# Low parts of the gating and GLU weights: a VectorE subtraction becomes a ScalarE negation and an accumulating DMA

## The chip, the cores and the metric

The kernel runs on one core of one Trainium2 chip. The metric is device time in microseconds (us) of one execution, the median over several runs. The engines are TensorE (PE in the profile; its weight loads are PEld), VectorE (DVE), ScalarE (ACT), GpSimd (POOL) and SyncE (SP). Sixteen DMA engines move data between HBM and SBUF for all queues.

## The reference

One decoder layer over 1024 prompt positions and 64 sample tokens (1088 columns), D_MODEL 1024, all in float32:

```
p     = rmsnorm(x) @ w_in                      # 1024 -> 512 (S5) + 512 (u) + 512 (v)
y     = gelu(Re(C h) + D u)                    # S5: 32 groups, 64 complex states, a scan over positions
o_s5  = y * sigmoid(y @ w_glu + b_glu)         # GLU, 512 x 512
v     = layernorm(gelu(p_v));  u = gelu(p_u)
o_cm  = u * (tril(W_s) v + b)                  # gating, 8 heads, chunks of 128 positions
x     = x + concat(rmsnorm(o_s5), rmsnorm(o_cm)) @ w_out
x     = x + (silu(h @ w_gate) * (h @ w_up)) @ w_down,  h = rmsnorm(x)
```

The last hidden states, the last v rows and a final RMSNorm are outputs too.

## The kernel before, in words

Activations lie with features on the 128 partitions and the 1088 columns in three chunks of 384, 384 and 320. Every large product is made of three matmuls on rounded parts: a float32 operand is split in a high part, `hi`, of type float32r, and a low part `lo = src - hi`. `mm3` (lines 150 to 152) adds `hi*hi`, `hi*lo` and `lo*hi` in one PSUM bank. So each weight tile is split once after it has been loaded. `split` does that in two instructions: ScalarE copies to `hi` (line 146) and VectorE subtracts (line 147). The two form the low part strictly one after the other, and `lo` is a tile that TensorE waits for.

`w_in` comes as six column quarters `q` of 256 columns, each in two halves of 512 rows. `load_q` (lines 239 to 245) loads a half of 512 KB to a raw tile of which three exist (`raw`, shared by most weight loads), and splits it. The halves live in three slots (`wqp`, tags `wqh` and `wql`; the tile `cwr` in the profile), so that the slot of a half is free only when TensorE has read another half for the last time. Quarters 0 and 1 are the S5 group's inputs (`s5_in`), 2 and 3 are the v columns (`v_quarter`, tile `pv`), 4 and 5 the u columns (`cm_out`, tile `pu`). In all of these the first half (k of 0 to 3) is read before the second (k of 4 to 7).

The S5 group is worked off in eight steps (`s5_a`, `s5_b`, `s5_c`): VectorE builds tables and scans, TensorE makes small products, and the halves of the partitions are swapped by DMA (`Sw`, `gw`). TensorE does the products of v and u between them, and VectorE the layer norm of v and the gating. When the last S5 step has stored its `ys`, four loads bring the result back by features (tile `g`, line 761, through `ys_d`), and the GLU begins (`glu`, tile `pg`). The GLU's weight tiles `wgh` and `wgl` lie in memory that the S5 steps have used, so they are written only then, from raw tiles that were loaded long before (lines 754 to 757). The output projection (`wo_tile`) and the feed-forward part follow.

The program is written as one stream, and a planner orders each engine's queue at build by estimated times of its instructions and by what is ready (`schedule_with_timeline_sim=True`); within a queue the chip keeps that order. All DMAs are issued by SyncE; GpSimd issues none.

Of the kernel before, what the change touches and what calls it, by code (L numbers as in the profile page):

```python
# [10 lines left out]
F32 = mybir.dt.float32  # L11
F32R = mybir.dt.float32r
I32 = mybir.dt.int32
AF = mybir.ActivationFunctionType
ALU = mybir.AluOpType
# [68 lines left out]
def layer_kernel(ctx: ExitStack, tc: tile.TileContext, A, O, dbg=None):  # L84
    nc = tc.nc
    V, S, P, PE, Q = nc.vector, nc.scalar, nc.gpsimd, nc.tensor, nc.sync
# [51 lines left out]
    def raw(name, shape):  # L138
        n = int(np.prod(shape))
        t = rawp.tile([128, 1024], F32, tag="raw", name=name, bufs=3)[:, :n]  # L140
        if len(shape) == 2:
            t = t.rearrange("p (a b) -> p a b", a=shape[0])
        return t

    def split(src, hi, lo, eng=None):
        S.activation(hi, src, AF.Copy)  # L146
        return (eng or V).tensor_tensor(lo, src, hi.bitcast(F32), ALU.subtract)  # L147

    def mm3(p, wh, wl, ah, al, start, stop):
        PE.matmul(p, wh, ah, start=start, stop=False)  # L150
        PE.matmul(p, wh, al, start=False, stop=False)  # L151
        return PE.matmul(p, wl, ah, start=False, stop=stop)  # L152
# [86 lines left out]
    def load_q(key, src, to=None):  # L239

        r = raw(f"w{key[0]}{key[1]}{key[2]}", (4, 256))
        Q.dma_start(r, src)
        h, l = to or [wqp.tile([128, 4, 256], F32R, tag=x, name=x) for x in ("wqh", "wql")]
        split(r, h, l)
        WQ[key] = (h, l)

    def load_wq(q):
        for half in range(2):
            load_q(("i", q, half), A["w_in"][q, :, 4 * half:4 * half + 4, :])
# [33 lines left out]
    def fm_group(q, c, tag="mm"):  # L283

        n0, n = CH[c]
        pp = [bank(f"pu{m}", tag)[:, :n] for m in range(2)]
        km = [(k, m) for k in range(8) for m in range(2)]
        for k, m in km if q == 0 else sorted(km, key=lambda x: x[1]):
            wh, wl = wq(q, k, slice(128 * m, 128 * m + 128))
            MM[q, c] = mm3(pp[m], wh, wl, xh[:, k, n0:n0 + n], xl[:, k, n0:n0 + n], k == 0, k == 7)  # L290
        return pp
# [14 lines left out]

    load_x(0, 0)
    load_q(("i", 0, 0), A["w_in"][0, :, 0:4, :])
    load_x(0, 1)
    load_q(("i", 0, 1), A["w_in"][0, :, 4:8, :])  # L310
    load_x(0, 2)
    load_x(0, 3)
# [298 lines left out]
    r = raw("bdr", (8, 64))  # L611
# [16 lines left out]
    r = raw("wsr", (8, 128))  # L628
# [4 lines left out]
    for q in range(2):  # L633
# [3 lines left out]
        for i in range(4):  # L637
            m, h = divmod(4 * q + i, 2)
# [6 lines left out]
    def v_quarter(q, j):  # L645
        p = bank("pv")
        for k in range(8):
            wh, wl = wq(q, k, slice(0, 256))
            mm3(p[:, 0:256], xh[:, k, tok(j)], xl[:, k, tok(j)], wh, wl, k == 0, k == 7)
        S.activation(v[:, j, 256 * (q - 2):256 * (q - 1)], p[:, 0:256], AF.Gelu_apprx_tanh, scale=r1c[:, j:j + 1])  # L650
# [101 lines left out]
    wgh = gl.tile([128, 4, W], F32R, name="wgh")  # L752
    wgl = gl.tile([128, 4, W], F32R, name="wgl")
    for i in range(2):
        r = raw(f"wg{i}", (2, W))
        Q.dma_start(r, A["w_glu"][:, 2 * i:2 * i + 2, :])
        split(r, wgh[:, 2 * i:2 * i + 2, :], wgl[:, 2 * i:2 * i + 2, :])
    G5 = []
    for m in range(4):
        g5 = gl.tile([128, 8, 136], F32, name=f"g5{m}")  # L760
# [10 lines left out]
    def glu(c):  # L771
        n0, n = CH[c]
        acc = ACC5[c] = gl.tile([128, 384], F32, tag="acc", name="acc", bufs=3)[:, :n]
        for m in range(4):
            p = bank("pg", "s5" if m % 2 else "mm")
            for k in range(4):
                mm3(p[:, :n], wgh[:, k, 128 * m:128 * m + 128], wgl[:, k, 128 * m:128 * m + 128],
                    xh[:, k, n0:n0 + n], xl[:, k, n0:n0 + n], k == 0, k == 3)
            sg = gl.tile([128, 384], F32, tag="sg", name="sg", bufs=2)[:, :n]
            S.activation(sg, p[:, :n], AF.Sigmoid, bias=gcol("bglu", m))  # L780
            for z, s_, q_ in tc2n(G5[m], n0, n, sg, accum_to(gl, acc, m == 0)):
                V.tensor_tensor(z, z, s_, ALU.mult)
                S.activation(q_, z, AF.Square)
            accum_end(acc, m == 0)
# [32 lines left out]
    i = 0  # L817
# [522 lines left out]
```

## Time and profile before

| | |
|---|---|
| median of 3 runs | 1118.43 us (1116.59 to 1118.62) |
| the profiled execution | 1114.1 us, span 1112.3 us |
| PE busy | 1055.7 us, 95% |
| DVE busy | 894.6 us, 80% |
| ACT busy | 436.8 us, 39% |
| POOL busy | 322.3 us, 29% |
| DMA moved | 131.20 MB, mean 118 GB/s |

The profiled execution is one that the hardware profiler recorded; its span runs from the first to the last instruction. Busy shares are means over stages with different limits. Matmuls are pipelined and their recorded durations overlap, so a busy TensorE is not one at its peak. In lists of waits, the name behind the arrow is what ended the idle time.

### The profile page before, as it was taken

What the parts mean: (1) busy time and instruction counts of PE and PEld (TensorE: products, weight loads), DVE (VectorE), ACT (ScalarE), POOL (GpSimd) and SP (SyncE); (2) the same over time, 40 slices, a digit from 0 to 9 for tenths busy, and PEclk for the clock granted to TensorE, in tenths of its full rate; (3) what the DMA queues carried; (4) which work ended last, traced back from release to release, by engine and by line L of the source; (5) the groups of instructions that cost most, each with busy time, mean ns of one, the idle gap of its engine ahead of it and who ended that gap; (6) DMA issues with size and microseconds to landing.
All of it is one profiled execution on the core that took longest, in us unless ns stands there. A gap on an engine that the chain in (4) does not pass through costs nothing.

```text
span 1112.3 us, 20465 instructions
## 1 busy us (share of the span) xinstructions
PE 1055.7 (95%) x7966; PEld 1028.5 (92%) x7966; DVE 894.6 (80%) x1820; ACT 436.8 (39%) x834; POOL 322.3 (29%) x287
## 2 busy tenths in 40 slices
PE   7899999979999899999999999999999899999995
PEld 6799998869999789999999999999998899899994
DVE  7988999898988996666666666666669879879998
ACT  7314423477444543233233233233244334424561
POOL 5010350000000435425425435335335221223220
PEclk9999999989999899999999999999999999999997
DMA  8341334364223113223223223223256715514304
GB/s 278 105 145 48 96 111 144 82 195 168 96 94 111 39 57 128 90 77 127 77 91 127 75 81 124 88 74 128 82 183 213 277 39 197 174 50 141 127 15 161
DMA packets 81520, 131.20 MB, mean 118 GB/s; under 512 B 8976, under 2 KB 60048, under 8 KB 81296
## 3 DMA queue, kind: packets, MB, share of 16 engines
q1 hardware_dynamic: 81424, 129.91, 36.0%
q8 instruction: 62, 1.02, 0.4%
q14 instruction: 34, 0.28, 0.1%
HBM read 90.43 MB, written 34.24 MB: 112 GB/s over the span
## 4 chain that ended last, share of the span: by engine, by line
PE 65%; DVE 18%; DMA 8%; issue 4%; ACT 3%; POOL 1%; SPq 0%; DVEq 0%; ACTq 0%; POOLq 0%
PE u L152 15%; PE u L150 15%; PE u L151 15%; DMA h<-hid_d 4%; PE po L152 3%; PE po L151 3%; PE po L150 3%; DVE xl L147 2%; PE pv L151 1%; PE pv L150 1%; PE pv L152 1%; DVE cwr L147 1%; DVE fb L147 1%; DMA gw<-gt 1%; PE pg L150 1%
## 5 line engine op out<-in xcount | busy, mean ns | idle before, releaser
L150 PE MATMUL u<-xh,h 128*128 128x272 f32 x516 | 149.1, 289 | 1.7 <-ACT h L146 1.5
L152 PE MATMUL u<-xh,h 128*128 128x272 f32 x516 | 148.5, 289 | 1.3 <-DVE h L147 1.3
L151 PE MATMUL u<-xl,h 128*128 128x272 f32 x516 | 148.7, 289 | 0.8 <-DVE xl L147 0.8
L150 PE MATMUL u<-xh,fb 128*128 128x272 f32 x382 | 110.7, 290 | 0.6 <-DVE x1r L1134 0.4
L151 PE MATMUL u<-xl,fb 128*128 128x272 f32 x382 | 110.6, 290 | 0.6 <-DVE xl L147 0.6
L152 PE MATMUL u<-xh,fb 128*128 128x272 f32 x382 | 110.3, 290 | 0.0
L1049 POOL TENSOR_TENSOR tS<-q,q 128x512 f32<-128x512 f32 x22 | 29.4, 1338 | 245.5 <-DVE h L914 145.9
L150 PEld LDWEIGHTS u<-xh,h 128*128 128x128 f32 x516 | 97.1, 188 | 2.4 <-ACT h L146 1.9
L152 PEld LDWEIGHTS u<-xh,h 128*128 128x128 f32 x516 | 96.9, 188 | 1.7 <-DVE h L147 1.7
L151 PEld LDWEIGHTS u<-xl,h 128*128 128x128 f32 x516 | 97.2, 188 | 1.0 <-DVE xl L147 1.0
L146 ACT ACTIVATE h<-q 128x512 fp32r<-128x512 f32 (+1 forms) x83 | 51.0, 615 | 80.7 <-PE u L151 75.2
L147 DVE TENSOR_TENSOR h<-q,h 128x512 fp32r<-128x512 f32 (+1 forms) x83 | 69.1, 834 | 7.0 <-ACT h L146 5.7
L151 PEld LDWEIGHTS u<-xl,fb 128*128 128x128 f32 x382 | 72.5, 190 | 0.9 <-DVE xl L147 0.9
L150 PEld LDWEIGHTS u<-xh,fb 128*128 128x128 f32 x382 | 72.3, 189 | 1.0 <-DVE x1r L1134 0.6
L152 PEld LDWEIGHTS u<-xh,fb 128*128 128x128 f32 x382 | 72.2, 189 | 0.1
L150 PE MATMUL pu<-xh,cwr 128*128 128x384 f32 (+1 forms) x192 | 65.6, 346 | 6.2 <-DVE us L303 6.2
L1087 ACT ACTIVATE st<-st 128x272 f32<-128x272 f32 x88 | 37.8, 431 | 72.1 <-DVE st L1109 34.5
L152 PE MATMUL pu<-xh,cwr 128*128 128x384 f32 (+1 forms) x192 | 64.9, 341 | 0.0
L151 PE MATMUL pu<-xl,cwr 128*128 128x384 f32 (+1 forms) x192 | 64.7, 338 | 0.0
L1054 POOL TENSOR_TENSOR tS<-tS,q 128x512 f32<-128x512 f32 x22 | 30.4, 1383 | 113.2 <-DVE h L147 60.5
L146 ACT ACTIVATE fb<-q 128x512 fp32r<-128x512 f32 (+1 forms) x64 | 38.7, 608 | 56.9 <-PE u L151 49.0
L150 PE MATMUL u<-cwr,h 128*128 128x272 f32 x189 | 55.1, 291 | 2.9 <-ACT cwr L146 2.3
(439 smaller groups left out, 3741.7 us busy)
## 6 DMA issues: line engine op xcount, KB each, us to landing
hid_d<-st SPq DMA_DIRECT2D x22, 952.0 KB, 4.2
h<-hid_d SPq DMA_DIRECT2D x28, 544.0 KB, 3.9
q<-in_w_gate_dram SPq DMA_DIRECT2D x22, 512.0 KB, 3.5
q<-in_w_up_dram SPq DMA_DIRECT2D x22, 512.0 KB, 3.5
q<-in_w_d_dram SPq DMA_DIRECT2D x16, 512.0 KB, 3.8
wo<-in_w_out_dram SPq DMA_DIRECT2D x14, 512.0 KB, 4.2
wi<-in_w_in_dram SPq DMA_DIRECT2D x12, 512.0 KB, 5.7
h<-hid_d SPq DMA_DIRECT2D x14, 408.0 KB, 3.1
```

Of the source, the lines that this page charges most:

```text
L146: S.activation(hi, src, AF.Copy)
L147: return (eng or V).tensor_tensor(lo, src, hi.bitcast(F32), ALU.subtract)
L150: PE.matmul(p, wh, ah, start=start, stop=False)
L151: PE.matmul(p, wh, al, start=False, stop=False)
L152: return PE.matmul(p, wl, ah, start=False, stop=stop)
L1049: P.tensor_tensor(tS, a21, a22, ALU.add)
L1054: P.tensor_tensor(tS, tS, a11, ALU.subtract)
L1087: S.activation(dst, src, AF.Silu)
```

## The change

For the four halves each of v and u (quarters 2 to 5, eight halves) and for the two halves of the GLU's weights, the low part is made in another way. ScalarE writes `hi` as before, then ScalarE writes `-hi` into `lo`, and then GpSimd issues a DMA that reads the weights from HBM once more and adds them to `lo`. VectorE's subtraction falls away for these ten. Quarters 0 and 1, the output projection and the activations keep `split`.

```
+    def wsplit_d(raw_, src, hi, lo):
+        S.activation(hi, raw_, AF.Copy)
+        S.activation(lo, hi.bitcast(F32), AF.Copy, scale=-1.0)
+        P.dma_start(lo, src, accum_op=ALU.add)
...
     def load_q(key, src, to=None):
         r = raw(f"w{key[0]}{key[1]}{key[2]}", (4, 256))
         Q.dma_start(r, src)
...
-        split(r, h, l)
+        if key[0] == "i" and key[1] >= 2:
+            wsplit_d(r, src, h, l)
+        else:
+            split(r, h, l)
...
     for i in range(2):
         r = raw(f"wg{i}", (2, W))
         Q.dma_start(r, A["w_glu"][:, 2 * i:2 * i + 2, :])
-        split(r, wgh[:, 2 * i:2 * i + 2, :], wgl[:, 2 * i:2 * i + 2, :])
+        wsplit_d(r, A["w_glu"][:, 2 * i:2 * i + 2, :], wgh[:, 2 * i:2 * i + 2, :], wgl[:, 2 * i:2 * i + 2, :])
```

## Rows read from the trace of the kernel before

**Rows 1.** Busy time by stretch: start:end, us; then PE, PEld, DVE, ACT, POOL, PEclk, DMA share, GB/s.
```profile
30.00:72.00 42.00, 35.78 (x200) 34.35 (x199) 38.92 (x152) 10.72 (x19) 4.37 (x18) 0.92 0.27 85
72.00:161.00 89.00, 88.93 (x699) 85.17 (x698) 81.28 (x185) 30.58 (x73) 24.08 (x21) 1.00 0.37 102
161.00:219.00 58.00, 56.41 (x418) 50.67 (x416) 52.80 (x119) 23.07 (x54) 4.80 (x9) 1.00 0.41 115
219.00:230.00 11.00, 7.15 (x45) 4.87 (x44) 9.94 (x20) 6.51 (x10) 0.00 (x0) 0.84 0.37 113
230.00:264.00 34.00, 27.15 (x149) 26.84 (x149) 31.75 (x78) 28.95 (x62) 0.00 (x0) 0.90 0.54 169
```

**Rows 2.** The chain that ended last, 30 to 230 us: start, us on it, what.
```profile
40.96 1.14 DVE cwr L147
...
72.23 0.51 DVE cwr L147
...
85.07 0.12 PE pv L150
...
138.90 0.17 PE pu L151
...
164.07 1.14 DVE cwr L147
```

**Rows 3.** Waits of TensorE, 30 to 75 us: us in total, times, longest.
```profile
PE pu L150 <- DVE us L303: 6.2, 2, 5.2
```

**Rows 4.** Groups by line on VectorE, 72 to 230 us, shapes kept apart.
```profile
L147 DVE TENSOR_TENSOR cwr<-wi,cwr 128x1024 fp32r<-128x1024 f32 x7 | 8.5, 1215 | 0.5 <-ACT cwr L146 0.4
```

**Rows 5.** The GLU's raw weight tile: ns min/median/max, first and last start.
```profile
L146 ACT ACTIVATE wgh<-wg x2: 1046/1046/1046, 230.1 to 231.0; 128x1024 fp32r<-128x1024 f32 x2
L147 DVE TENSOR_TENSOR wgl<-wg,wgh x2: 1216/1217/1218, 232.2 to 233.8; 128x1024 fp32r<-128x1024 f32 x2
```

**Rows 6.** Timeline: split of the first and the last second half.
```profile
69.30 1.06 ACT L146 ACTIVATE cwr<-wi 128x1024 fp32r<-128x1024 f32 x1 [5.42 <-PE pu L151]
...
72.15 1.22 DVE L147 TENSOR_TENSOR cwr<-wi,cwr 128x1024 fp32r<-128x1024 f32 x1
...
178.12 1.04 ACT L146 ACTIVATE cwr<-wi 128x1024 fp32r<-128x1024 f32 x1
...
181.48 1.21 DVE L147 TENSOR_TENSOR cwr<-wi,cwr 128x1024 fp32r<-128x1024 f32 x1
```

**Rows 7.** Busy time by stretch around the GLU's start, columns as in the first group.
```profile
230.00:236.00 6.00, 0.00 (x0) 0.00 (x0) 6.00 (x13) 5.97 (x9) 0.00 (x0) 0.88 0.92 268
236.00:242.00 6.00, 5.15 (x18) 5.15 (x19) 5.98 (x15) 4.77 (x15) 0.00 (x0) 0.55 1.19 328
```

**Rows 8.** Timeline around the GLU's start: TensorE, then ScalarE.
```profile
218.76 0.31 PE L152 MATMUL pu<-xh,cwr 128*128 128x320 f32 x1
...
236.85 2.61 PE L150 MATMUL pg<-xh,wgh 128*128 128x384 f32 x7 [6.95 <-ACT xh L146]
...
239.58 0.52 PE L152 MATMUL pg<-xh,wgl 128*128 128x384 f32 x1
...
236.28 1.39 ACT L146 ACTIVATE xh<-g 128x384 fp32r<-128x384 f32 x4
238.10 1.39 ACT L146 ACTIVATE xh<-g 128x384 fp32r<-128x384 f32 x4 [0.44 <-DMA g<-ys_d]
```

**Rows 9.** DMA issues: KB each, median us to landing; the issue's own ns.
```profile
wi<-in_w_in_dram SPq DMA_DIRECT2D x12, 512.0 KB, 5.7
g<-ys_d SPq DMA_DIRECT2D x4, 544.0 KB, 7.2
L242 SPq DMA_DIRECT2D wi<-in_w_in_dram x12: 328/386/1387, 2.1 to 162.5; - x12
```

**Rows 10.** Timeline of GpSimd: one shape beside a busy VectorE.
```profile
148.14 1.29 POOL L710 TENSOR_TENSOR cvp<-v,lgb 128x512 f32<-128x512 f32 x1 [1.45 <-DVE v L658]
...
154.91 3.72 POOL L710 TENSOR_TENSOR cvs<-v,lgb 128x512 f32<-128x512 f32 x1 [2.53 <-DMA mb<-mb]
```

## The prediction, made before the changed kernel ran

> **What bounds the kernel now.** I read busy time by stretch first, then the chain that ended last, then the waits, and only then single instructions. Everything that the change touches lies between 40 and 245 us; what comes later is moved as a block. By stretch [rows 1] TensorE is full from 72 to 161 us (88.9 of 89.0) and nearly so to 219 (56.4 of 58.0); VectorE is close behind with 91% in both (81.3 of 89.0, 52.8 of 58.0). The chain [rows 2] says which of them counts where. Around 41 us it runs over VectorE, and a subtraction of a `w_in` half is on it with 1.14 us; TensorE waits there for VectorE, 5.2 us at the longest [rows 3]. From 85 us on the chain's pieces are matmuls, 0.12 us for one of `pv` and 0.17 us for one of `pu` [rows 2]. After 161 us it is VectorE's again: the subtraction at 164.07 is on it in full. TensorE ends its last `pu` at 219 us, and then idles before the GLU, 6.95 us in one piece [rows 8], while the last S5 step ends and its result comes back through HBM: from 236 to 242 us the DMA engines are as busy as they get (share 1.19, 328 GB/s) and TensorE has a mean clock of 0.55, so near its lower level of 1.2 GHz, after having idled [rows 7]. So there are three stages with different limits: VectorE before 72 us, TensorE with VectorE close behind it to 161, VectorE with S5 transfers to 230, and transfers around the GLU's start.
>
> **What the change removes.** Ten subtractions of 128x1024. One is the piece at 41 us. Seven lie between 72 and 230 us, 8.5 us in sum at 1.215 us each [rows 4]. Two are the GLU's, 1.217 us each, from 232.2 us on [rows 5].
> - The first: on the chain, TensorE waits at its end. Gain 1.1 us (bounds 0 and 1.2).
> - The five between 72 and 161 us (the first of them at 72.15 [rows 6]): 6.1 us of VectorE's time while TensorE has no gap. On the chain stands 0.51 us of them [rows 2], since the first of them delays a store that the S5 steps start from. What TensorE's order doesn't let through is no gain; but the S5 steps are also VectorE's work, and they end the stage at 230, after TensorE's last `pu`. Bounds 0.5 and 6.1; VectorE's 91% is nearer to the full than to nothing, TensorE's 100% to nothing, so I take half, 3.0 us.
> - The two at 164.07 and 181.48 (the latter with no idle of VectorE before it [rows 6]): on VectorE's part of the chain, 2.4 us (bounds 1.1 and 2.4).
> - The GLU's two: nothing. VectorE is busy there (6.00 of 6.00 us), but the stage waits for the `g` loads: the second one's split is released by the DMA [rows 7, 8].
> Sum of gains 1.1 + 3.0 + 2.4 = 6.5 us (1.6 to 9.7). The end of the S5 steps can move that far: there are 11 us between TensorE's last `pu` and 230 us.
>
> **What it adds.**
> - *Ten negations on ScalarE*, priced like the copy to `hi` of the same shape, 1.05 us [rows 5, 6]. From 72 to 219 us ScalarE is busy for a third (30.6 of 89, 23.1 of 58), so that idle time hides them; what is queued behind one on ScalarE is at worst an S5 evacuation, which TensorE and VectorE then wait for. Bounds 0 and 3.2 us (three that hit one); I take 0.5.
> - *Ten issues on GpSimd*, where no issue stands in this trace. An issue took SyncE 0.39 us [rows 9], and a GpSimd operation on 128x512 1.3 us [rows 10]: these are the bounds, and I take 1.3 us, being GpSimd's own. GpSimd is 27% busy to 161 us (24.1 of 89.0) and 8% after [rows 1], so the issues themselves cost nothing. But an issue waits for its negation, and the layer norm's small powers and the S5 states' copies are queued behind it on GpSimd, with VectorE and TensorE waiting for those; I count this with the low parts that come late.
> - *The low part comes later.* Now it ends 3.0 us after `hi` (70.36 to 73.37) and 3.5 us after it (179.16 to 182.69) in the first and the last of the four second halves [rows 6]. After the change: negation 1.05, issue 0.4 to 1.3, and the transfer, for which the nearest rows are a plain load of the same bytes, 5.7 us, and the loads of `g`, 7.2 us [rows 9]. That makes 7.1 to 9.6 us, so 4 to 6 us later. The four first halves have slots that come free early, or are read late. The four second halves are needed almost at once, since their slot is released by the matmuls just ahead. The cover: TensorE has the first-half products of the next groups, in four PSUM banks 4 x 12 matmuls, 5.8 us at 0.12 or 8.2 at 0.17 [rows 2]. If the planner puts these ahead, nothing is lost; if it keeps today's order, there are 12 matmuls (1.4 or 2.0 us) and TensorE stands still for up to 4 x 6 us. I take nothing, because interleaving is what this planner can do in a full stage; 24 us is the other end.
> - *The GLU's start.* The two accumulating DMAs can be issued from about 232 us, after `hi` is there, amid the `g` loads. They bring 2 x 0.524 MB more from HBM; at the 328 GB/s that the engines moved then [rows 7] this is 3.2 us of all sixteen, while `g` waits. Twice that, 6.4 us, if adding costs the engines a second pass over the bytes. `wgl` is first needed at 239.58 [rows 8], so lateness up to about 240 is covered, and the two negations on ScalarE (2.1 us, ScalarE 5.97 of 6.00 busy [rows 7], `g` split at 236.28 right behind other work [rows 8]) overlap with waiting for `g`. Bounds 1.0 and 6.4; a plain load is the nearest row, so I take 3.2.
>
> Such a transfer has no row here. The Trainium skill (DMA: Bandwidth & Descriptors, Anatomy of one DMA) gives about 2.0 us and bytes over 436 GB/s for a DMA issued by GpSimd, an estimate of 3.2 us for one of these; by it the low parts would be only some 2 us later than now and the sum would stay what it is. No run here shows it yet.
>
> **Sum.** -6.5 + 0.5 + 0 + 3.2 = -2.8 us against the profiled execution of 1114.1 us (span 1112.3 and 1.8 outside it), so 1111.3. The median of the runs shown lies 4.3 us above that execution, at 1118.43; the same step from there gives 1115.6 us. What a measurement of this kernel can tell from no change is about 0.2%, 2.2 us.
>
> **The rivals.**
> - *Late second halves.* TensorE waits for `lo` in a stage where it is full, and S5 products queued behind the waiting matmul wait too. For it: TensorE has no gap in which a wait could vanish before 161 us [rows 1]. Against: the 48 matmuls of cover. Price: four times 5 us (the middle of 4 to 6), half of it covered, +10 us: 1115.6 + 10 = 1125.6. It decides from the point where a transfer lands more than the cover of 5.8 us after TensorE has begun the first half.
> - *The GLU takes it back.* The accumulating transfers cost twice their bytes at a time when the engines are full [rows 7]: 6.4 in place of 3.2, sum +0.4 us: 1118.8, no change.
> - *GpSimd starved.* The same add of 128x512 took GpSimd 1.29 us at one time and 3.72 us at another beside a busy VectorE [rows 10], 2.4 us more. If issues stretch so, the four second halves lose 4 x 2.4 = 9.7 us, and the waits behind them on GpSimd grow as well: about 1125.3. [...]
> - *Everything is let through.* VectorE is the limit for the S5 steps all along, 9.7 us of gains, 0.5 lost on ScalarE, and 1.0 us at the GLU, because a GLU that starts earlier finds ScalarE free: -8.2, 1110.2.
>
> **How the numbers follow.** The forecast has 0.40 (0.28 faster, 0.11 within 0.2%, 0.01 slower), its own range 1112 to 1119. Late second halves 0.25 (0.05 same, 0.20 slower); the GLU 0.13 (0.03 faster, 0.06 same, 0.04 slower); GpSimd starved 0.10, all slower; everything let through 0.12, all faster. Faster is 0.28 + 0.03 + 0.12 = 0.43, same 0.11 + 0.05 + 0.06 = 0.22, slower 0.01 + 0.20 + 0.04 + 0.10 = 0.35. Cases of both signs hold most of the chance, so the range has to reach to both: from 1109.5, just under everything let through, to 1127.5, which holds the larger part of the two slow cases and leaves those with less cover out.
>
> **What would show it.** Right: no subtraction of `wi` but those of quarters 0 and 1; the last S5 store some 5 us earlier than now, at the end of the stretch to 230 us; TensorE's `pv` and `pu` without new waits for `cwr`; the first `pg` less than 4 us later after that store than now. Wrong in the late halves: waits of TensorE `pv` or `pu` for a DMA into `cwr`, four of 3 us or more. Wrong at the GLU: `g` landing over 3 us later after its issue, or `pg` waiting for a DMA into `wgl`. Wrong at GpSimd: gaps of several us between the end of a negation and its issue. The prediction falls as a whole if the planner orders TensorE's queue very differently: then single stretches can't be compared, only the ends of stages.

## The result, and the profile after

The kernel before took 1118.53 us, the changed one 1127.82 us (medians of four runs each): ratio 1.0088, 95% interval 1.0066 to 1.0110. So the change costs 9.8 us by the ratio (the medians differ by 9.3), where a gain of 2.8 us was forecast, and the time lies just over the upper end of the range (1127.5). The profiled execution of the changed kernel took 1126.44 us with a span of 1124.7. Its lines stand 6 to 9 below the old ones: `mm3` is L156 to L158, `wsplit_d` L151 (`hi`), L152 (`-hi`) and L153 (the accumulating DMA).

Busy time by stretch, after, in the columns of [rows 1]:

```profile
30.00:72.00 42.00, 36.30 (x205) 35.19 (x205) 37.77 (x151) 12.23 (x21) 4.23 (x17) 0.92 0.34 93
72.00:161.00 89.00, 84.69 (x659) 79.78 (x657) 74.05 (x174) 35.97 (x79) 24.18 (x28) 1.00 0.55 133
161.00:219.00 58.00, 54.66 (x395) 49.53 (x396) 47.53 (x113) 22.38 (x52) 3.73 (x10) 0.97 0.52 137
219.00:230.00 11.00, 10.04 (x78) 8.96 (x75) 8.86 (x19) 2.87 (x6) 0.00 (x0) 1.00 0.19 49
230.00:264.00 34.00, 22.26 (x118) 20.44 (x117) 26.92 (x61) 28.60 (x53) 1.71 (x2) 0.80 0.75 215
```

VectorE did lose its work: 7.2 us of busy time less from 72 to 161 us, 5.3 less to 219. Only 8.5 of these 12.5 us are the seven subtractions; the rest is work that now comes later. So the relief became idle time. TensorE is not full any more in these two stretches (84.7 for 88.9, 54.7 for 56.4), and the DMA engines are at 0.55 and 0.52 for 0.37 and 0.41. From 230 to 264 us TensorE works 5 us less than before.

The waits of TensorE from 30 to 75 us, and then from 72 to 260 us (us in total, times, longest):

```profile
PE pu L156 <- DVE us L312: 5.7, 2, 3.7
...
PE pg L156 <- ACT xh L146: 7.0, 1, 7.0
PE pg L158 <- DMA wgl<-in_w_glu_dram: 4.7, 1, 4.7
PE sb L518 <- DMA U<-us_d: 4.5, 2, 3.3
PE pu L158 <- DMA cwr<-in_w_in_dram: 1.1, 1, 1.1
...
PE pv L157 <- DMA cwr<-in_w_in_dram: 0.4, 1, 0.4
```

The longest wait before the first `pv` fell from 5.2 us [rows 3] to 3.7, the two of its kind together from 6.2 to 5.7. The two waits for a low part of `w_in` (`cwr`) make 1.5 us together. The large new ones are for `U`, an input of the S5 steps, and for `wgl`. VectorE waits for the S5 steps' transfers in the same way (72 to 231 us):

```profile
DVE gt L585 <- DMA gw<-gt: 11.9, 6, 3.8
DVE PT L500 <- DMA bc<-in_bc_dram: 6.3, 1, 6.3
DVE Ss L562 <- DMA Sw<-Ss: 5.1, 3, 2.6
```

In the kernel before these three were 7.0, 3.3 and 0.5 us. The chain that ended last now runs over such transfers for longer. From 30 to 230 us, `gw` had 5.2% of it before and has 9.7% now, and `Sw` has 6.0%, while matmuls of `pv`, 20% before, are no longer among its large parts. Some of its longest pieces from 30 to 260 us (start, us, what):

```profile
107.65 5.94 DMA Sw<-Ss
...
171.86 5.09 DMA gw<-gt
...
190.68 7.04 DMA gw<-gt
...
239.93 9.85 DMA wgl<-in_w_glu_dram
```

No subtraction of [rows 4] is left: the split of a half is now, by ScalarE's timeline, one that answers to the first of [rows 6], and its transfer by GpSimd's:

```profile
69.95 1.06 ACT L151 ACTIVATE cwr<-wi 128x1024 fp32r<-128x1024 f32 x1 [5.39 <-PE pu L157]
71.04 1.06 ACT L152 ACTIVATE cwr<-cwr 128x1024 fp32r<-128x1024 f32 x1
```
```profile
72.40 0.86 POOL L153 DMA_DIRECT2D cwr<-in_w_in_dram  x1 [3.95 <-ACT cwr L152]
```

The accumulating DMA itself (line L153: its issues in ns, min/median/max, then us to landing; and the DMA issues by kind, KB each and median us to landing):

```profile
L153 POOL DMA_DIRECT2D cwr<-in_w_in_dram x8: 853/860/1077, 42.8 to 190.1; - x8
L153 POOL DMA_DIRECT2D wgl<-in_w_glu_dram x2: 856/856/856, 239.9 to 240.9; - x2
DMA to landing us min/median/max: 5.9/7.4/12.1
```
```profile
wi<-in_w_in_dram SPq DMA_DIRECT2D x12, 512.0 KB, 4.7
cwr<-in_w_in_dram POOLq DMA_DIRECT2D x8, 512.0 KB, 7.2
g<-ys_d SPq DMA_DIRECT2D x4, 544.0 KB, 7.2
wgl<-in_w_glu_dram POOLq DMA_DIRECT2D x2, 512.0 KB, 11.0
```

An issue takes GpSimd 0.86 us, at most 1.08, beside a VectorE that is 83% busy, and follows its negation by 0.3 us; so the stretching of [rows 10] did not befall these ten issues. A transfer takes 7.2 us where the plain load of the same bytes takes 4.7, and 11.0 at the GLU's start (medians; 5.9 to 12.1 over all ten).

There, the timeline shows ScalarE, GpSimd and TensorE (start, us, engine, line, what, idle time before it):

```profile
236.39 1.99 ACT L151 ACTIVATE wgh<-wg 128x1024 fp32r<-128x1024 f32 x2
...
238.59 1.99 ACT L152 ACTIVATE wgl<-wgh 128x1024 fp32r<-128x1024 f32 x2
240.48 1.38 ACT L146 ACTIVATE xh<-g 128x384 fp32r<-128x384 f32 x4
```
```profile
239.93 1.80 POOL L153 DMA_DIRECT2D wgl<-in_w_glu_dram  x2 [22.50 <-ACT wgl L152]
```
```profile
241.04 2.61 PE L156 MATMUL pg<-xh,wgh 128*128 128x384 f32 x7 [7.01 <-ACT xh L146]
243.44 1.65 PE L157 MATMUL pg<-xl,wgh 128*128 128x384 f32 x7
249.81 0.69 PE L158 MATMUL pg<-xh,wgl 128*128 128x384 f32 x1 [4.72 <-DMA wgl<-in_w_glu_dram]
250.30 0.52 PE L156 MATMUL pg<-xh,wgh 128*128 128x384 f32 x1
```

The last `ys_d` store leaves at 231.66 us. `wgh`, which came 0.6 us behind that store (229.51, then 230.1 [rows 5]), comes 4.7 us behind it; the negations follow, the transfers leave at 239.93, 8.3 us after the store, and TensorE stands for `wgl` until 249.81. Busy time by stretch, answering to [rows 7]:

```profile
236.00:242.00 6.00, 0.96 (x3) 0.96 (x4) 5.16 (x12) 6.00 (x11) 1.71 (x2) 0.60 1.20 318
242.00:248.00 6.00, 3.10 (x13) 2.78 (x11) 4.76 (x14) 5.97 (x15) 0.00 (x0) 0.78 1.07 317
248.00:254.00 6.00, 4.19 (x13) 4.19 (x14) 5.39 (x13) 2.89 (x8) 0.00 (x0) 0.50 0.78 193
```

The DMA engines stay at 1.07 or more for 12 us instead of 6. TensorE idles a second time, and its granted clock falls a second time, to 0.50, the lower level of 1.2 GHz.

### The profile page after: what moved, and what is told of

The parts are those of the page before. It is cut to its first block, busy times and chain, and to the rows that moved or that the text cites. A ratio compares the mean times of both kernels' runs of the same rounds, so it can differ in the third digit from the quotient of the medians.

```text
span 1124.7 us, 20481 instructions
## 1 busy us (share of the span) xinstructions
PE 1057.1 (94%) x7966; PEld 1029.3 (92%) x7966; DVE 885.1 (79%) x1810; ACT 446.3 (40%) x844; POOL 321.3 (29%) x297
## 4 chain that ended last, share of the span: by engine, by line
PE 63%; DVE 18%; DMA 10%; issue 5%; ACT 2%; SPq 1%; POOL 1%; DVEq 0%; ACTq 0%; POOLq 0%
PE u L158 16%; PE u L156 16%; PE u L157 16%; DMA h<-hid_d 4%; PE po L156 3%; PE po L157 3%; PE po L158 3%; DMA gw<-gt 2%; DVE xl L147 1%; PE ss L170 1%; PE pu L156 1%; PE pu L157 1%; PE pu L158 1%; DMA Sw<-Ss 1%; DVE gt L568 1%
## 5 line engine op out<-in xcount | busy, mean ns | idle before, releaser
L158 PE MATMUL u<-xh,h 128*128 128x272 f32 x516 | 149.2, 290 | 1.9 <-DVE h L147 1.9
L156 PE MATMUL u<-xh,h 128*128 128x272 f32 x516 | 149.3, 290 | 1.2 <-ACT h L146 1.0
L156 PE MATMUL u<-xh,fb 128*128 128x272 f32 x382 | 110.5, 289 | 0.6 <-DVE x1r L1143 0.4
L158 PE MATMUL u<-xh,fb 128*128 128x272 f32 x382 | 110.3, 289 | 0.2 <-DVE fb L147 0.2
L158 PEld LDWEIGHTS u<-xh,h 128*128 128x128 f32 x516 | 97.4, 189 | 2.5 <-DVE h L147 2.5
L156 PEld LDWEIGHTS u<-xh,h 128*128 128x128 f32 x516 | 97.4, 189 | 1.7 <-ACT h L146 1.2
L156 PEld LDWEIGHTS u<-xh,fb 128*128 128x128 f32 x382 | 72.2, 189 | 1.0 <-DVE x1r L1143 0.6
L158 PEld LDWEIGHTS u<-xh,fb 128*128 128x128 f32 x382 | 72.0, 189 | 0.4 <-DVE fb L147 0.4
L156 PE MATMUL pu<-xh,cwr 128*128 128x384 f32 (+1 forms) x192 | 66.8, 352 | 5.7 <-DVE us L312 5.7
L158 PE MATMUL pu<-xh,cwr 128*128 128x384 f32 (+1 forms) x192 | 64.4, 339 | 1.1 <-DMA cwr<-in_w_in_dram 1.1
L156 PE MATMUL u<-cwr,h 128*128 128x272 f32 x189 | 55.5, 294 | 3.1 <-ACT cwr L146 2.4
```

## The experiments

To compare stages, I take points of each profiled execution, in us from its first `pv` matmul (the start-up before it varies by 3 us between executions): the last `ys_d` store, the last `pu`, the first `pg`, the first and the last `po`, each at its start. The ratio is that of the times, with its interval; the names are explained below.

| kernel | last store | last `pu` | first `pg` | first `po` | last `po` | ratio to before |
|---|---|---|---|---|---|---|
| before (two executions) | 158.0, 157.3 | 147.3, 146.6 | 165.4, 164.8 | 192.3, 192.0 | 291.5, 291.2 | 1 |
| changed | 159.6 | 159.0 | 168.9 | 202.2 | 301.3 | 1.0088 (1.0066 to 1.0110) |
| 1 `w_glu` alone | 157.1 | 146.6 | 166.2 | 197.5 | 296.7 | 1.0036 (1.0017 to 1.0055) |
| 2 `w_in` alone | 158.7 | 158.2 | 166.3 | 196.4 | 295.6 | 1.0063 (1.0045 to 1.0080) |
| 3 all negated, no transfer | 150.1 | 155.1 | 157.5 | 180.8 | 291.5 | 0.9988 (0.9977 to 0.9999) |
| 4 `w_in` negated, no transfer | 150.0 | 155.1 | 157.0 | 180.6 | 290.6 | 1.0000 (0.9980 to 1.0019) |
| 5 as 4, accumulating to scratch | 151.8 | 154.1 | 158.6 | 185.4 | 291.9 | 1.0014 (1.0000 to 1.0027) |
| 6 as 4, plain loads to scratch | 150.9 | 153.2 | 157.8 | 183.3 | 289.5 | 0.9988 (0.9972 to 1.0004) |
| 7 `w_in` subtracted on GpSimd | 151.4 | 156.2 | 159.0 | 182.0 | 292.4 | 1.0045 (1.0028 to 1.0063) |
| 8 as 2, `wg` loads by GpSimd | 153.3 | 156.3 | 162.3 | 190.2 | 295.9 | 1.0044 (1.0027 to 1.0061) |
| 9 before, `wg` loads by GpSimd | 157.3 | 147.0 | 165.1 | 192.1 | 291.3 | 1.0026 (1.0010 to 1.0042) |
| 10 `w_glu` negated, no transfer | 157.7 | 147.0 | 166.9 | 194.6 | 293.7 | 1.0012 (0.9995 to 1.0029) |
| 11 first halves alone | 153.6 | 147.6 | 160.7 | 188.5 | 287.6 | 0.9976 (0.9959 to 0.9993) |
| 11 again | 158.5 | 152.6 | 165.6 | 193.9 | 293.0 | 0.9991 (0.9976 to 1.0006) |
| 12 second halves alone | 151.7 | 151.9 | 160.7 | 188.5 | 294.0 | 1.0048 (1.0031 to 1.0064) |
| 13 second halves to scratch | 157.0 | 151.3 | 163.3 | 189.3 | 289.6 | 1.0030 (1.0015 to 1.0044) |
| 14 as 3, no loads of `x1q` | 150.2 | 155.1 | 157.5 | 180.9 | 284.0 | 0.9945 (0.9931 to 0.9958) |
| 15 before, no loads of `x1q` | 157.1 | 146.5 | 164.7 | 191.6 | 290.9 | 0.9997 (0.9985 to 1.0010) |

One caution for reading it: kernel 11 was profiled twice, and its last store came 4.9 us apart, where ScalarE had waited 12.1 us for the store of `us_d` in place of 9.9 and TensorE 2.9 us for ScalarE. A single difference of that size in a kernel with added transfers proves nothing; I use differences that repeat or that the times confirm.

Two things more. The table ends at the last `po`, but the kernels go on to differ behind it. In the 85 us after it TensorE does 570 matmuls in the kernel before (569 in 9, 15 and the changed kernel), but 554 in kernel 3, 532 in 4, 533 in 14, 559 in 12 and only 517 in 13 (the feed-forward part's first products, 0.13 us each; before and 13, in the columns of [rows 1]):

```profile
363.10:448.10 85.00, 77.89 (x570) 75.57 (x570) 69.42 (x108) 35.02 (x61) 38.66 (x28) 0.94 0.22 73
363.60:448.60 85.00, 73.96 (x517) 71.44 (x516) 67.69 (x106) 33.32 (x58) 39.85 (x28) 0.90 0.21 68
```

And the planner orders TensorE's queue anew for most edits. By the tiles that the matmuls write, the order up to the first `pg` is one and the same in the kernel before, 1, 9, 10 and 15; in 2 and the changed kernel; in 3 and 14; in 5 and 6. It differs between 2 and 4, between 4 and 5, and between 12 and 13. So those pairs compare a transfer together with the order that goes with it.

**The parts (1, 2, 3).** Theory A: the loss is made at the GLU's start. Rival B: in the stage of v, u and S5. Theory C: the transfers eat VectorE's relief. Rival D: the relief is worth nothing.

```
1:  load_q keeps  split(r, h, l);           w_glu keeps  wsplit_d(...)
2:  load_q keeps  wsplit_d(...) for q >= 2; w_glu keeps  split(...)
3:  all as in the change, and in wsplit_d
-        P.dma_start(lo, src, accum_op=ALU.add)
```

In 3 the low parts stay `-hi`, so the products are not the reference's; the other instructions are the same, in an order of their own.

> The accumulating DMA only for the two halves of the GLU's weights; all of w_in by the subtraction on VectorE, as before. Theory A (the loss is made at the GLU's start: in the changed kernel the low parts landed 11 us after their issue, and TensorE waited 4.7 us for them): slower than before by 6 to 9 us, 1124 to 1128 us. Rival B (the loss is made in the stage of v, u and S5, where the last matmul of u ended 12 us later): within 2 us of before.

> The accumulating DMA only for the eight halves of w_in; the GLU's weights by the subtraction on VectorE. Theory A: within 3 us of before, 1117 to 1122 us, since the store of the last S5 step came only 2 us later in the changed kernel. Rival B: slower by 6 us or more.

> The changed kernel without the accumulating DMAs: the low parts are -hi, so the products of v, u and the GLU are not the reference's. What is left is the relief of VectorE and ten more instructions on ScalarE. Theory C (the added transfers eat the relief, since the S5 steps' own small transfers wait beside them): faster than before by 4 us or more, 1109 to 1115 us. Rival D (VectorE's relief is worth nothing, since the S5 steps wait for transfers and TensorE's order): 1116 to 1120 us.

Beside them the kernel before was profiled again (span 1117.1 us):

> The kernel before once more, with a profile, to see which times of stages repeat. If they do, the last S5 store comes at 229.5 us and the first matmul of the GLU at 236.9, both within 1.5 us.

The losses add up: 0.36% and 0.63% give 0.99% against 0.88% measured. So neither A nor B holds alone. Kernel 3 divides the other pair: the S5 steps end 7 to 8 us earlier without transfers, as C says, yet the time is only 1.3 us better, in D's range. Both needed a second look: where the transfers cost, and where a lead of 7 us goes.

**The transfers of `w_in` (4, 5, 6).** 4 leaves out the eight transfers only. 5 and 6 then put the same traffic back, behind the same negations, into a tile that nobody reads (the products are not the reference's in all three). The tile is one only, so ScalarE waits twice for the transfer before, 8.3 us in sum in 5 and 5.5 in 6: they show the traffic's cost with something on top.

```
 4:     wsplit_d(r, src, h, l)                        # two activations, no DMA
 5, 6:
+       S.activation(scr[:, :, :1], l.bitcast(F32)[:, :, :1], AF.Copy)
 5: +   P.dma_start(scr, src, accum_op=ALU.add)
 6: +   P.dma_start(scr, src)
```

> The eight w_in halves with the negation and without the accumulating transfer (their low part is then -hi, so the products aren't the reference's); w_glu keeps its subtraction. Theory E (the eight transfers cost the time, whatever the cause): 1115 to 1118.5 us, last store of ys_d some 6 to 8 us after-first-pv earlier than before, us_d store landing near 4.5 us, U near 3. Rival G (the negations, or the other order that the planner makes without the subtractions, cost it): 1121 to 1125, like the run with the w_in transfers alone.

> As the kernel with the eight negations and no transfer into the low part, but GpSimd issues after each negation an accumulating transfer of the same 512 KB into a scratch tile that nobody reads (a one-column ScalarE copy orders it behind the negation). So TensorE never waits for such a transfer. Theory E1 (contention: the transfers slow the S5 steps' own transfers and loads): 1121 to 1125, last ys_d store about 158 us after the first pv, us_d landing near 7.5 us and U near 5. Rival E2 (lateness: TensorE's order has to wait for low parts that land late): 1115 to 1119, ys_d store near 150 us after the first pv.

> The same scratch transfers, but plain loads in place of accumulating ones. If moving the bytes is what costs: as slow as the accumulating scratch run, within 2 us. If adding costs the DMA engines more than moving: 2 us or more faster than that run, and its landing near a plain load's 5 us instead of 7.

Without transfers the 0.63% are gone (1.0000): the loss of `w_in` belongs to the transfers and the order that goes with them, not to the negations. As mere traffic, accumulating ones cost 0.14% (0.00 to 0.27), plain ones nothing measurable. The signs of Theory E1 are missing in 5: the store of `us_d` lands after 5.1 us and `U` after 2.9, where kernel 2 has 7.9 and 5.3, and the last store comes at 151.8. (In 6 they land after 6.4 and 5.2 us, and the time is no longer for it.) The intervals of 5 and 6 overlap, so that adding costs more than moving is likely by the landing (7.5 against 5.7 us), but not settled by the time. Traffic alone is thus the smaller part of the loss of all eight here.

**First and second halves (11, 12, 13).**

```
 11: -  if key[0] == "i" and key[1] >= 2:
     +  if key[0] == "i" and key[1] >= 2 and key[2] == 0:
 12: +  ... and key[2] == 1:
 13: as 5, with key[2] == 1 (low parts of the second halves stay -hi)
```

> Accumulating transfers for the four first halves of quarters 2 to 5 only; the second halves and w_glu by subtraction. If the low parts that come late in the second halves make the loss (the rival named in the prediction): no loss, 1115.5 to 1118.5. If every transfer costs the same: half of the loss of the run with all eight, 1119.5 to 1122.

> Accumulating transfers for the four second halves of quarters 2 to 5 only; first halves and w_glu by subtraction. The run with the first halves alone came out 0.24% faster than before, that with all eight 0.63% slower. If the second halves make the loss: ratio 1.005 to 1.010, last ys_d store 157 us or more after the first pv, TensorE waits for cwr of 1 us and more. If it takes both (the sum of the traffic): 0.998 to 1.002, the store near 154.

> The four second halves by negation (their low part stays -hi, not the reference's product), with an accumulating transfer of the same bytes into a scratch tile that nobody reads; first halves and w_glu by subtraction. The traffic is that of the run with the second halves alone, but no engine waits for it. If the loss of the second halves is made by waiting for their low parts, and by the order that the planner gives the queues because they come late: ratio 0.996 to 1.000. If it is made by the traffic itself at these times: as that run, 1.004 to 1.010.

> The kernel with the accumulating transfers of the four first halves alone, once more, beside the other two on one chip. If its gain holds: ratio 0.996 to 0.999. If it was chance: 0.999 to 1.002.

The first halves cost nothing: 0.9976 and 0.9991 in two measurements on two chips, at best a gain of 0.2%. This is the only version with the reference's products that came out under the kernel before, and its second interval holds 1. The second halves make the loss (1.0048). But TensorE hardly waits for them: in kernel 12 the wait for `cwr` is 0.8 us in sum. Nor does the loss arise among the S5 steps, as I had expected: in kernel 12's one profile their last store comes at 151.7, some 6 us earlier than before. The loss arises in the projection, where TensorE waits for VectorE's work on `x1q`, the residual that is the subject of kernels 14 and 15 (225 to 300 us):

```profile
PE po L156 <- DVE x1q L851: 4.2, 1, 4.2
```

Kernel 13, the same transfers with nobody waiting, took 0.30% more than before, between the two forecasts. That is no price of the traffic: up to the last `po` it is 1.6 to 1.9 us ahead of the kernel before, and it loses its time after that, in the 53 matmuls that it lacks above, when no added transfer runs any more. So how the loss of the second halves divides between traffic, late low parts and the order that the planner builds around them stays open: 12 and 13 differ by less than their intervals, and four scratch transfers in 13 can't be shown to cost more than eight in 5.

**SyncE's queue (8, 9).** In the profile after, one place of that order can be named. SyncE from 160 to 172 us, and its longest wait there:

```profile
163.26 0.84 SPq L721 DMA_DIRECT2D out_cvs_dram<-cvs  x1
164.19 5.50 SPq L765 DMA_DIRECT2D wg<-in_w_glu_dram  x2
169.78 0.38 SPq L488 DMA_DIRECT2D U<-us_d  x1
170.25 0.38 SPq L598 DMA_DIRECT2D ys_d<-ys  x1
170.68 0.42 SPq L494 DMA_DIRECT2D bc<-in_bc_dram  x1
171.20 0.61 SPq L571 DMA_DIRECT2D gw<-gt  x1
```
```profile
SPq L765 <- DMA out_cvs_dram<-cvs: 4.2, 1, 4.2
```

The second load of `wg` waits 4.2 us for the raw tile that the store of `cvs` still reads. The S5 step's load of `U`, its store, its `bc` and its swap `gw` stand behind it; `U` leaves at 169.78 and TensorE waits 3.3 us for it at 175. In the kernel before that wait was 1.1 us, and `U` left between the two loads, at 165.30. In kernel 2 it is 4.1 us again.

```
-        Q.dma_start(r, A["w_glu"][:, 2 * i:2 * i + 2, :])
+        P.dma_start(r, A["w_glu"][:, 2 * i:2 * i + 2, :])
```

> The kernel with the eight w_in accumulating transfers alone, and the two loads of the GLU's raw weights issued by GpSimd in place of SyncE. Theory H: in the run with the eight transfers the second of these loads waits 4.1 us on SyncE (164 to 169 us) for the store of cvs to land, and U's load, the ys_d store, bc and gw of an S5 step stand behind it. Without that: TensorE's wait for U near 175 us under 1 us in place of 2.6, last ys_d store near 155 us after the first pv in place of 158.7, 1119 to 1121.5 us. Rival I (the transfers' contention finds another place): last ys_d store at 158 again, 1122.5 to 1125.

> Control: the kernel before with the two loads of the GLU's raw weights issued by GpSimd. SyncE waits only 1.1 us for the same store there: 1117 to 1119.5 us, no change. If this issue alone gains, 1114 to 1116.5.

In kernel 8 the wait is gone, `U` leaves at 163.12, and the last store comes 5.4 us earlier than in 2 (153.3 for 158.7). The time gains little (1.0044 for 1.0063, intervals that overlap), while the control loses 0.26% by the same edit. So by these profiles, one of each kernel, the block in SyncE's queue is a part of the delay of the S5 steps, but the time doesn't show it: kernel 8 has a 4.4 us wait for `x1q` later on, which is the next point.

**Where a lead goes (14, 15).** In kernels 3, 4 and 7 the GLU starts 6 to 8 us earlier, and the last `po` ends where it ended before. The wait that takes most of it in kernel 3 (225 to 300 us), what these loads themselves wait for, and SyncE's loads there:

```profile
PE po L155 <- DVE x1q L850: 5.3, 1, 5.3
```
```profile
SPq L836 <- DVE xl L147: 1.9, 1, 1.9
```
```profile
270.29 0.33 SPq L247 DMA_DIRECT2D wo<-in_w_out_dram  x1
272.64 4.72 SPq L836 DMA_DIRECT2D x1q<-in_xT_dram  x7
```

And SyncE in the kernel before:

```profile
SPq L828 <- DVE xl L147: 14.0, 1, 14.0
```
```profile
263.25 4.59 SPq L828 DMA_DIRECT2D x1q<-in_xT_dram  x8
```

`x1q`, the residual that VectorE adds to the projection, lies in memory of the gating, so its loads wait for the gating's last low part (`xl`). The order of TensorE's queue is another here, S5 products ahead of those of u (presumably since the planner sees the S5 steps ready sooner): the last `pu` comes 8 us later than before, the gating ends later, and the loads leave 9.4 us later. The same wait is 5.8 us in kernel 7, 3.9 in 5 and 5.0 in 6, but only 1.2 in 4, where TensorE stands 2.9 us for ScalarE's splits instead and starts the feed-forward part more slowly. Kernels 14 and 15 replace these loads by memsets on GpSimd, so that six blocks of the residual are left out.

```
-            Q.dma_start(t, A["xT"][:, 2 + a:2 + b, NH * c:NH * c + NH])
+            P.memset(t, 0.0)
```

> The kernel with all ten negated and no accumulating transfer, whose S5 steps end 7 us earlier but whose time is only 0.12% under the kernel before; its eight loads of the residual x1q are replaced by memsets on GpSimd (the residual of six blocks is left out). Theory L: the lead is given back because x1q lies in the gating's memory, its loads leave SyncE only after the gating's last low part (272.6 us in place of 263.3), and TensorE waits 5.3 us for the VectorE additions on it. Without these loads' 6 us: that wait under 1.5 us and a ratio of 0.994 to 0.997. Rival M (another limit follows at once, VectorE or ScalarE in the projection): 0.998 to 1.000.

> Control: the kernel before with the same eight loads replaced by memsets. TensorE doesn't wait for x1q there: 0.999 to 1.001.

```profile
PE po L155 <- DVE x1q L850: 0.7, 1, 0.7
```

In kernel 14 the wait falls from 5.3 to 0.7 us and the ratio from 0.9988 to 0.9945; the same edit changes the kernel before by nothing (0.9997). So VectorE's relief was worth some 6 us, as a whole, and the late residual took most of it, 0.43% or 4.8 us, in this order of the queues.

**The GLU without its transfers (10).** `w_glu` by negation, its low part left at `-hi`; `w_in` by subtraction.

> Only w_glu by negation, without its two accumulating transfers (its low part is then -hi, not the reference's product); w_in by subtraction as before. Theory J (the transfers beside the loads of g cost the 4 us of the run with w_glu alone): 1116.5 to 1119.5, loads of g near 7 us, first pg 7 to 8 us after the last ys_d store. Rival K (two negations on ScalarE ahead of the split of g cost it): 1120 to 1123, first pg 9 us or more after that store.

1.0012 against 1.0036 with the transfers: by the middle values two thirds of the GLU's 4.0 us come with the transfers, but the intervals overlap, and what is left is not told from nothing. In kernel 1 the four loads of `g` land 9.6 us after their issue, in kernel 10 after 7.3, before after 7.2 [rows 9], as Theory J has it. Rival K has its sign too: the first `pg` comes 9.1 us after the last store in kernel 1 and 9.2 in 10, where J expected 7 to 8 and the kernel before has 7.4 and 7.5. So these 1.7 us come with the negations. From the first `pg` to the first `po` it is 31.3 us in 1 and 27.7 in 10 (before 26.9 and 27.2), so 3.6 us come with the transfers. Both hold in part.

**The subtraction on GpSimd (7).** `split(r, h, l, P)` for the eight halves: no transfer, no VectorE.

> The kernel before with the eight w_in subtractions on GpSimd in place of VectorE: no negation, no transfer, the reference's result. Theory D (VectorE's relief before 230 us is given back later): 1116 to 1120. Rival (the relief is worth its 5 to 6 us where no transfer takes it): 1111 to 1114. If GpSimd takes over 3 us for one and blocks VectorE meanwhile: 1120 or more.

One took 2.97 us in the mean, 5.6 at most. The S5 steps end 6 us earlier, TensorE waits 5.8 us for `x1q`, and the time is 0.45% worse. The lead is lost in the same place as in 3; why it ends worse than 3 was not followed up.

## Why the prediction was wrong

**The first subtraction** (gain 1.1): not contradicted, and not shown in full. The longest wait at its end fell by 1.5 us, the two waits together by 0.5.

**The other seven** (gain 3.0 + 2.4): at the place that I named the gain was there, and larger, within the bounds of 1.6 to 8.5 of these two terms. Without transfers the last store comes 7.1 to 8.0 us earlier in kernels 3, 4 and 14. The step that failed is a sentence of the first part: "what comes later is moved as a block". It isn't a block. The projection needs data from two sides, the GLU and the gating, and only one of them became earlier, the other later. In time the relief is worth 1.3 us (kernel 3) instead of 6.

**The transfers in the full stage** had no term in the sum. I asked whether TensorE would wait for low parts, and put the cost at 0, with 24 us as the other end. The cover held: 1.5 us of waits (2.8 in kernel 2). But 4.2 MB beside the S5 steps' own transfers, with what the planner and SyncE's queue make of them, moved the S5 end from 150 (kernel 4) to 158.7 us (kernel 2). By the times it is 0.63% of 1118, 7.0 us, with nothing measurable from the first halves. So the step that failed is that the cost of a transfer was taken to be TensorE's wait for it, and nothing else. Against the kernel before, kernel 2's S5 steps end only 0.7 to 1.4 us later; 3 us more go between the first `pg` and the first `po` (30.1 us for 26.9 and 27.2), with the last `pu` 11 us later than before. The rival *Late second halves* had the right halves and nearly the right price, and the wrong mechanism: no four waits of 3 us, but late `U`, `gw` and `bc` with all eight transfers, and a late `x1q` with the second halves alone. What makes them late, the traffic or the changed order, stays open. *Everything is let through* falls by kernels 3 and 4, *GpSimd starved* by the issue of 0.86 us. The Trainium skill (SBUF — State Buffer, Who interferes with whom) tells of GpSimd's DMAs that a VectorE operation starves of port time for their descriptors; no issue of an accumulating transfer took longer than 1.19 us in any run here.

**The GLU's start** (+3.2, bounds 1.0 and 6.4): alone it costs 4.0 us (0.36%, 1.9 to 6.1), near the term. But the mechanism was wrong for the changed kernel. The term has `g` waiting for the added bytes and the lateness of `wgl` covered up to about 240 us. There `g` landed after 7.2 us, as before, and TensorE stood 4.7 us for `wgl`. I had the issues start at about 232 us; they start at 239.93, since gating work and a split of `wo` that waits 1.2 us for its load stand ahead of `wgh` on ScalarE, and the two negations behind it. And a transfer took 11.0 us there. In all, from the last store to the first `po` are 42.6 us, before 34.3 and 34.7, so 8 us more in this profile; kernel 2, without these transfers, has 37.7. TensorE also idled twice, and its granted clock fell twice, to 0.60 and 0.50. In kernel 1 alone `g` landed late (9.6 us) and nothing waited for `wgl`, as the term had it. The negations, which the prediction let overlap with waiting for `g`, cost 1.7 us up to the first `pg` in kernels 1 and 10.

**The price of one transfer**: I bounded it by 5.7 and 7.2 us, and it is 7.2. The estimate by the Trainium skill (DMA: Bandwidth & Descriptors, Anatomy of one DMA), 3.2 us, is less than half of that; the measurement decides.

The sum by what was measured: the whole edit of `w_in`, its relief included, costs 7.0 us (kernel 2), that of `w_glu` 4.0 (kernel 1), together 11.0, each uncertain by 2 us, against 9.8.

## What to carry to other kernels

Before crediting an engine's relief to the end time, ask what the later stage needs from elsewhere: here a lead of 7 us met a buffer that another branch released later than before. Price a transfer that is added to a full stage not only by who waits for it (1.5 us here, where the edit of `w_in` cost 7.0): look also at the transfers that it runs beside, at the in-order queue that issues them, and at the order that the planner makes with it. Compare stages to the end of the kernel before a difference in time is put to one of them. Work that can move to a DMA was cheap here where its result has slack, as in the first halves, and dear in the second halves, which are wanted at once; why these are dear stays open.

## What the runs showed of the hardware that was not expected

- An accumulating DMA of 512 KB from HBM took 7.2 us to land (median of eight), a plain load of the same bytes 4.7 in the same kernel; into scratch, both issued by GpSimd, 7.5 against 5.7.
- Beside the loads of `g` an accumulating transfer took 11.0 us in the changed kernel and 7.9 in kernel 1, where those loads landed 2.4 us later than before.
- A subtraction of 128x1024 took GpSimd 2.4 to 5.6 us, VectorE 1.2 [rows 4].
